# Differential attention in a written-out order, with pieces of the following products between its steps and fewer conditioning sums beside it

## Chip, cores and metric

The kernel runs on one core of one Trainium2 chip. The metric is the device time of one execution in microseconds (us), taken as the median of three runs.

## What is computed

The reference is two transformer blocks in a row on 256 tokens of width 1024, all in float32. The first block is a sparse-attention and convolution mixer and a SwiGLU. The second block has two layers of three sublayers: SwiGLU, mixer, SwiGLU; the mixer of its layer 0 is differential attention, that of layer 1 a gated recurrence. Each sublayer is modulated by shift, scale and gate vectors that are products of a conditioning vector `c` (1024) with a 1024x1024 matrix each, 24 vectors in all. Differential attention, cut to what matters here:

```python
q, k, v = jnp.split(h @ w_qkv, 3, axis=-1)
q = rms_norm(q.reshape(B, S, H, 2, hd), q_gain) * (hd ** -0.5)
k = rms_norm(k.reshape(B, S, H, 2, hd), k_gain)
...
s = jnp.einsum('bhcqd,bhckd->bhcqk', q_blk, kt).astype(jnp.float32) + bias[None, :, None]
s = jnp.where(dist >= 0, s, -jnp.inf)
p = jax.nn.softmax(s, axis=-1)
a = p[:, :, 0] - lam_full * p[:, :, 1]
return jnp.einsum('bhqk,bhkv->bhqv', a, vt)
...
o = rms_norm(o, subln_gain) * (1.0 - lambda_init)
return o.reshape(B, S, H * dv).astype(h.dtype) @ w_o
```

There are 8 heads with two 64-wide query and key halves each, and values of 128.

## The kernel before

**Products.** A float32 product is made of three matmuls on fp32r halves: weight high by activation high, weight low by activation high, weight high by activation low. `Stream` brings every weight matrix in chunks of 128x2048 through a pool of five raw buffers. For each half of a chunk ScalarE copies the high part (`whi`, L200) and VectorE subtracts it (`wlo`, L213); `Stream.next` hands out the two halves of a chunk, splits a number of halves ahead (`ahead`) and issues the loads of later chunks (`loads`) on SyncE's queue.

**Conditioning sums.** The 24 vectors come from 88 columns of 1 MB (`adaraw`) and the first block's own. `ADA_PLAN` is a table of (chunk number, columns loaded by then). `Stream.next` calls `ada_step` with the chunk number plus 8: at most one more column is loaded, into the same five raw buffers, and the sums of one earlier column are made, two VectorE passes over 128x1024 (L550, or L548 for the first). When four columns of a vector are there, `reduce` turns the sum on TensorE (L570 for a gate, L573 for a shift or scale) and VectorE takes it from PSUM (L579, L581).

**Order.** Between `order(True)` and `order(False)` instructions keep, on every engine, the order in which the Python code issues them; elsewhere the tile framework's list scheduler reorders them by its own costs. The first block, all SwiGLUs and the first part of the recurrence are in written order. `diff_attention` (L1673) calls `order(False)` at its start; `finish` (L795) puts the written order back on for the last half of the output product.

**The attention stage.** It has four groups `i` of two heads. The SwiGLU before it ends with the first group's query/key product (`rows_first`). For each group, `normed` squares the product `ps_qk` on ScalarE (`qsq`, L1693), sums on VectorE (`qss`, L1695), takes the power -1/2 on GpSimd (L630), multiplies (`qk`, L1699), turns on TensorE (`ps_qkT`, L1704), and ScalarE writes `qn` and `kn` (L1707). Then for each 128 queries `t` and each half `e`: scores on TensorE (`ps_s`, L1726), bias and row maximum on VectorE (L1729), exponentials with row sums on ScalarE (L1734); after both halves the difference `a` on VectorE (L1737 to L1741), turned on TensorE (`ps_aT`, L1744) and copied by ScalarE (`aT`, L1745). `rows_half` makes the next group's query/key product, and later the two halves of the values (`ps_v`), each from two weight chunks. Per half of the values, `ps_o` (L1755) and `head_norm` follow: square, sum, power, multiply, turn (`ps_oT`, L1794) and split; then the output product `ps_do` from four chunks (`out_product`, `finish`).

Of the kernel before, what the change touches and what calls it, by code (L numbers as in the profile page):

```python
# [413 lines left out]
class Net:  # L414
# [85 lines left out]
    ADA_PLAN = ((0, 0), (8, 0), (14, 12), (36, 24), (56, 36), (76, 48), (93, 60), (126, 72), (159, 84), (184, 84), (204, 88))  # L500
# [170 lines left out]
    def half_pieces(self, name, done):  # L671
        acc = [self.psum("acc", f"{name}{t}") for t in range(2)]
        xh, xl = self.h
        for j in range(2):
            parts = self.W.next(ahead=1)
            for k in range(4):
                f = 4 * j + k
                for t in range(2):
                    self.rows_mm([acc[t]], parts[k // 2], t, (xh[:, f], xl[:, f]), f == 0, f == KT - 1, (k % 2) * 512)
                if k == 2:  # L680
                    self.W.split_to(2 * self.W.at + 1)
                if f == KT - 1:
# [40 lines left out]
    def rows_part(self, acc, lhs, ks, first):  # L723

        parts = self.W.next()
        for a, k in enumerate(ks):
            for t in range(2):
                self.rows_mm(acc[t], parts[a], t, lhs(k), first and a == 0, False)

# [942 lines left out]
    def diff_attention(self, bias_pool, end, scale, fill):  # L1672
        nc, T, tc, W = self.nc, self.T, self.tc, self.W  # L1673
        with ExitStack() as es:
# [10 lines left out]
            s0 = m1.tile([P, 2, 8], F32, name="s0")  # L1685
            acc, base = self.started
            self.ada_step(base + 8)
            self.ada_step(base + 9)
            self.order(False)
            for i in range(4):  # L1690
                def normed(t, ps):
                    sq = self.w512("qsq")
                    nc.scalar.activation(sq, ps, AF.Square)  # L1693
                    ss = m2.tile([P, 8], F32, name="qss")
# [3 lines left out]
                    y = self.w512("qk").rearrange("p (a b) -> p a b", a=8)  # L1698
                    nc.vector.tensor_tensor(out=y, in0=ps.rearrange("p (a b) -> p a b", a=8),  # L1699
                                            in1=ss[:, :, None].to_broadcast([P, 8, 64]), op=ALU.mult)  # L1700
                    y = y.rearrange("p a b -> p (a b)")
                    pt = self.psum("t", "ps_qkT")
                    for k in range(4):
                        nc.tensor.transpose(pt[:, k * P:(k + 1) * P], y[:, k * P:(k + 1) * P], self.ident)  # L1704
                    pt = pt.rearrange("p (a b) -> p a b", a=4)
                    for dst, src, gn in ((qn, pt[:, :2], qg), (kn, pt[:, 2:], kg)):
                        nc.scalar.activation(dst[:, 2 * i:2 * i + 2, t * P:(t + 1) * P], src, AF.Copy, scale=gn)  # L1707

                if i == 0:
                    for t in range(2):  # L1710
                        normed(t, acc[t])
                else:
                    self.rows_half("ps_qk", normed)
                for t in range(2):
                    n = (t + 1) * P
                    pa = self.psum("t", "ps_aT")
                    s = [None] * 2
                    s1 = m2.tile([P, 2], F32, name="ds1")
                    for e in range(2):

                        ps = self.psum("b", "ps_s").rearrange("p (a b) -> p a b", a=2)[:, :, :n]
                        s[e] = self.w512("s").rearrange("p (a b) -> p a b", a=2)[:, :, :n]
                        nm = m2.tile([P, 2], F32, name="dnm")
                        for k in range(2):
                            h = 2 * i + k
                            nc.tensor.matmul(ps[:, k], qn[64 * e:64 * e + 64, h, t * P:(t + 1) * P], kn[64 * e:64 * e + 64, h, :n],  # L1726
                                             start=True, stop=True, tile_position=(64 * e, 0))
                        for k in range(2):
                            nc.vector.tensor_tensor_reduce(out=s[e][:, k], in0=ps[:, k], in1=bias[:, 2 * i + k, S - n:], scale=1.0,  # L1729
                                                           scalar=GONE, op0=ALU.add, op1=ALU.max, accum_out=nm[:, k:k + 1])  # L1730
                        nc.vector.tensor_scalar(out=nm, in0=nm, scalar1=-1.0, scalar2=None, op0=ALU.mult)
                        for k in range(2):
                            h = 2 * i + k
                            nc.scalar.activation(s[e][:, k], s[e][:, k], AF.Exp, bias=nm[:, k:k + 1],  # L1734
                                                 accum_out=s0[:, t, h:h + 1] if e == 0 else s1[:, k:k + 1])

                    nc.vector.reciprocal(s1, s1)  # L1737
                    nc.vector.scalar_tensor_tensor(out=s1, in0=s0[:, t, 2 * i:2 * i + 2], scalar=nlam, in1=s1, op0=ALU.mult, op1=ALU.mult)
                    for k in range(2):
                        a = self.w256("a")[:, :n]  # L1740
                        nc.vector.scalar_tensor_tensor(out=a, in0=s[1][:, k], scalar=s1[:, k:k + 1], in1=s[0][:, k], op0=ALU.mult, op1=ALU.add)  # L1741
                        for b in range(t + 1):
                            c = k * (t + 1) + b
                            nc.tensor.transpose(pa[:, c * P:(c + 1) * P], a[:, b * P:(b + 1) * P], self.ident)  # L1744
                    nc.scalar.copy(aT[:, 2 * i:2 * i + 2, t:2 * t + 1], pa[:, :2 * n].rearrange("p (a b c) -> p a b c", a=2, b=t + 1))  # L1745
            v = m1.tile([P, 2, D], F32, name="v", tag="v")
            oh, ol = m1.tile([P, KT, S], F32R, name="oh", tag="qn"), m1.tile([P, KT, S], F32R, name="ol", tag="kn")
            for g in range(2):
                self.rows_half("ps_v", lambda t, ps: nc.scalar.copy(v[:, t, g * 512:(g + 1) * 512], ps))
                for t in range(2):  # L1750
                    ps = self.psum("b", "ps_o")
                    for e in range(4):
                        h = 4 * g + e
                        for b in range(t + 1):
                            nc.tensor.matmul(ps[:, e * P:(e + 1) * P], aT[:, h, t + b], v[:, b, h * P:(h + 1) * P],  # L1755
                                             start=b == 0, stop=b == t)
# [260 lines left out]
```

## Time and profile before

| | |
|---|---|
| runs, us | 1455.15, 1457.65, 1460.42; median 1457.65 |
| profiled execution | 1461.74 us, its span 1459.9 us, granted TensorE clock 0.992 |
| busy share of the span | TensorE 97%, VectorE 75%, ScalarE 49%, GpSimd 3% |
| DMA | 61.8% of 16 engines, 230 GB/s from HBM |

TensorE (PE) is busy nearly all of the span, so a gain has to come from stretches where it waits or runs at its lower clock. A busy PE is modelled from pipelined matmuls: what a matmul costs is read from the distance of starts or from the time of a whole train, not from its own duration.

### The profile page before, as it was taken

Reading aid. Unit: us, or ns where it says so; the run is one execution under the profiler, and the core shown is the slowest. Engines: PE = TensorE matmul, PEld = TensorE weight load, DVE = VectorE, ACT = ScalarE, POOL = GpSimd, SP = SyncE. Lnnn points to the kernel's source line nnn. Section 1 sums busy time; section 2 is a strip of 40 time slices with the busy share of each in tenths; the row PEclk is TensorE's granted clock in tenths of the full one; section 3 lists DMA queues with packets and bytes.
Section 4 is the critical chain, followed back from the end, with each engine's and each line's share of the span. In section 5 each row is a group of like instructions: output and inputs, shape, how many; then the busy total and the mean of one; then the engine's idle time right before and its main releaser. Section 6 shows DMA issues by size and latency. Waiting matters only on the chain.

```text
span 1459.9 us, 22646 instructions
## 1 busy us (share of the span) xinstructions
PE 1409.4 (97%) x9154; PEld 1258.5 (86%) x9154; DVE 1095.0 (75%) x1691; ACT 709.0 (49%) x1217; POOL 47.2 (3%) x45
## 2 busy tenths in 40 slices
PE   7999999999999999889999999999998999999998
PEld 6875889998899897667999998999987998899997
DVE  4889797778797678889776668866676998765555
ACT  4544534444444446565544445444455675454442
POOL 0001000000000000122000000000000001000000
PEclk9999999999999999999999999999999999999999
DMA  7866588774588875766476764766653244266640
GB/s 280 329 271 231 212 348 309 270 296 179 193 332 337 327 283 188 253 224 221 148 314 233 279 256 159 301 260 255 232 187 143 91 145 170 90 222 247 235 173 30
DMA packets 51353, 337.87 MB, mean 231 GB/s; under 512 B 5760, under 2 KB 7552, under 8 KB 13104
## 3 DMA queue, kind: packets, MB, share of 16 engines
q1 hardware_dynamic: 51104, 336.35, 61.8%
q8 instruction: 72, 1.18, 0.3%
q14 instruction: 33, 0.27, 0.1%
q10 hardware_dynamic: 144, 0.07, 0.0%
HBM read 335.33 MB, written 1.06 MB: 230 GB/s over the span
## 4 chain that ended last, share of the span: by engine, by line
PE 78%; DVE 12%; ACT 3%; issue 3%; POOL 2%; DMA 1%; SPq 0%; POOLq 0%; DVEq 0%; ACTq 0%
PE ps_dn L692 19%; PE ps_up L654 13%; PE ps_up L656 13%; PE ps_up L653 13%; DVE wlo L213 2%; PE ps_up L888 2%; PE ps_wo L708 2%; PE ps_att L692 2%; DVE adacc L550 1%; POOL qss L630 1%; PE ps_up L901 1%; PE ps_do L692 1%; ACT whi L200 1%; PE ps_c L1150 1%; PE ps_g L692 1%
## 5 line engine op out<-in xcount | busy, mean ns | idle before, releaser
L213 DVE TENSOR_TENSOR wlo<-raw,whi 128x1024 fp32r<-128x1024 f32 (+2 forms) x414 | 484.8, 1207 | 48.9 <-ACT whi L200 48.3
L200 ACT CAST whi<-raw 128x1024 fp32r<-128x1024 f32 (+2 forms) x414 | 412.7, 1037 | 130.1 <-issue 44.1
L654 PE MATMUL ps_up<-xh,wlo 128*128 128x256 f32 x1600 | 392.4, 283 | 1.2 <-DVE wlo L213 1.2
L653 PE MATMUL ps_up<-xh,whi 128*128 128x256 f32 x1600 | 393.5, 284 | 0.0
L654 PEld LDWEIGHTS ps_up<-xh,wlo 128*128 128x128 f32 x1600 | 306.1, 191 | 4.4 <-DVE wlo L213 1.6
L653 PEld LDWEIGHTS ps_up<-xh,whi 128*128 128x128 f32 x1600 | 305.9, 191 | 3.3 <-ACT g L1001 0.9
L656 PE MATMUL ps_up<-xl,whi 128*128 128x256 f32 x1600 | 224.4, 283 | 0.0
L656 PEld LDWEIGHTS ps_up<-xl,whi 128*128 128x128 f32 x1600 | 206.2, 192 | 0.0
L550 DVE SCALAR_TENSOR_TENSOR adacc<-adaraw,cact,adacc 128x1024 f32<-128x1024 f32 x154 | 197.3, 1281 | 4.5 <-ACT adacc L545 1.6
L1001 ACT ACTIVATE g<-ps_up 128x256 f32<-128x256 f32 x100 | 38.4, 384 | 317.9 <-PE ps_up L656 317.9
L692 PE MATMUL ps_dn<-whi,hh 128*128 128x512 f32 x440 | 174.0, 395 | 0.0
L692 PE MATMUL ps_dn<-wlo,hh 128*128 128x512 f32 x440 | 172.7, 393 | 0.0
L1003 DVE TENSOR_TENSOR hu<-ps_up,g 128x256 f32<-128x256 f32 x100 | 42.2, 422 | 154.5 <-ACT g L1001 154.3
L692 PE MATMUL ps_dn<-whi,hl 128*128 128x512 f32 x440 | 140.7, 394 | 0.0
L692 PEld LDWEIGHTS ps_dn<-whi,hl 128*128 128x128 f32 x440 | 82.6, 188 | 18.6
L692 PEld LDWEIGHTS ps_dn<-whi,hh 128*128 128x128 f32 x440 | 83.1, 189 | 17.0 <-issue 0.2
L692 PEld LDWEIGHTS ps_dn<-wlo,hh 128*128 128x128 f32 x440 | 82.8, 188 | 17.3 <-issue 0.2
L637 DVE TENSOR_TENSOR hl<-hu,hh 128x256 fp32r<-128x256 f32 x100 | 42.5, 425 | 47.2 <-ACT hh L636 47.2
L636 ACT CAST hh<-hu 128x256 fp32r<-128x256 f32 x100 | 40.7, 407 | 61.9 <-DVE hu L1003 61.9
L630 POOL TENSOR_TENSOR rstd<-rstd,mhalf 128x1 f32<-128x1 f32 x16 | 10.0, 626 | 867.4 <-DVE rstd L303 642.6
L369 ACT ACTIVATE xh<-ps_tr,vcol,modA 128x128 fp32r<-128x128 f32 x48 | 18.0, 456 | 31.4 <-PE ps_tr L358 25.7
L1921 PE MATMUL ps_l<-hX 128*128 128x128 f32 x224 | 29.8, 276 | 0.2 <-DVE hX L1906 0.2
(340 smaller groups left out, 1869.3 us busy)
## 6 DMA issues: line engine op xcount, KB each, us to landing
raw<-in_up_dram SPq DMA_DIRECT2D x110, 1024.0 KB, 6.1
adaraw<-in_ada_dram SPq DMA_DIRECT2D x88, 1024.0 KB, 5.7
raw<-in_down_dram SPq DMA_DIRECT2D x55, 1024.0 KB, 6.8
adas<-in_ada_s_dram SPq DMA_DIRECT2D x8, 1024.0 KB, 4.9
raw<-in_w_qk_dram SPq DMA_DIRECT2D x8, 1024.0 KB, 7.1
raw<-in_w_att_dram SPq DMA_DIRECT2D x8, 724.0 KB, 6.2
wraw<-in_w_conv_dram SPq DMA_DIRECT2D x8, 512.0 KB, 11.0
gate<-in_ada_b_dram SPq DMA_DIRECT2D x8, 512.0 KB, 7.8
```

What stands on the lines that cost most here:

```text
L200: net.nc.scalar.copy(hi[:, :n], src)
L213: self.net.nc.vector.tensor_tensor(out=lo[:, :n], in0=src, in1=hi.bitcast(F32)[:, :n], op=ALU.subtract)
L550: nc.vector.scalar_tensor_tensor(out=acc, in0=raw[:, k], scalar=c[:, 2 * j + k:2 * j + k + 1], in1=acc, op0=ALU.mult, op1=ALU.add)
L636: nc.scalar.copy(hi, src)
L637: nc.vector.tensor_tensor(out=lo, in0=src, in1=hi.bitcast(F32), op=ALU.subtract)
L653: mm(o, hi[:, at(k)], xh[:, k], start=k == 0, stop=False)
L654: mm(o, lo[:, at(k)], xh[:, k], start=False, stop=False)
L656: mm(o, parts[k // 4][0][:, at(k)], xl[:, k], start=False, stop=k == KT - 1)
L692: mm = lambda *args, **more: self.nc.tensor.matmul(*args, **more, **kw)
L1001: self.last_silu = nc.scalar.activation(g, ps[:, :S], AF.Silu)
L1003: nc.vector.tensor_tensor(out=u, in0=ps[:, S:], in1=g, op=ALU.mult)
L1921: nc.tensor.matmul(pd[:, o:o + P], x, x, start=True, stop=True)
```

## The change

`diff_attention` no longer calls `order(False)`: the whole stage keeps the order of the code. `normed` is cut into `begin` and `turn`, the rest of a group into `scores` and `weights`, the part per values half into `averaged` and `ended` (`head_norm` now yields once, after the power). A query/key, value or output product is issued in eight pieces of six matmuls (`half_pieces`, which also splits weights between its pieces, and `rows_pieces`), and `plan` names the step that follows a piece. `ADA_PLAN` is flatter from chunk 76 to 94 and steeper after; the reduction of vector 16 moves from the attention to the SwiGLU behind it, and that of vector 19 one SwiGLU further. The parts that are only regrouped are cut.

```diff
-    ADA_PLAN = ((0, 0), (8, 0), (14, 12), (36, 24), (56, 36), (76, 48), (93, 60), (126, 72), (159, 84), (184, 84), (204, 88))
+    ADA_PLAN = ((0, 0), (8, 0), (14, 12), (36, 24), (56, 36), (76, 48), (86, 52), (94, 56), (131, 70), (160, 84), (184, 84), (204, 88))
...
-            parts = self.W.next(ahead=1)
+            parts = self.W.next(ahead=1, loads=3)
...
+    def rows_pieces(self, acc, lhs, ks, first):
 
         parts = self.W.next()
         for a, k in enumerate(ks):
             for t in range(2):
                 self.rows_mm(acc[t], parts[a], t, lhs(k), first and a == 0, False)
+                yield
...
-            self.order(False)
-            for i in range(4):
-                def normed(t, ps):
...
+            def begin(i):
+                for t in range(2):
                     sq = self.w512("qsq")
...
                     self.power(ss, ss)
...
+            def turn(i, t):
+                ss, ps = sums.pop((i, t)), accs[i][t]
...
+            def scores(i, t):
...
+            def weights(i, t):
...
+            def qk(i):
+                accs[i] = {}
+                return self.half_pieces("ps_qk", accs[i].__setitem__)
+
+            def value(g):
+                return self.half_pieces("ps_v", lambda t, ps: nc.scalar.copy(v[:, t, g * 512:(g + 1) * 512], ps))
+
+            def run(stream, plan):
+                for p, _ in enumerate(stream):
+                    for f, *args in plan.get(p, ()):
+                        f(*args)
...
+            for i in range(4):
+                begin(i)
...
+                plan = {2: [(turn, i, 0)], 4: [(turn, i, 1), (scores, i, 0)], 5: [(scores, i, 1)], 7: [(weights, i, 0)]}
+                if i:
+                    plan[1] = [(weights, i - 1, 1)]
+                run(qk(i + 1) if i < 3 else value(0), plan)
...
+            ended = lambda g, t: next(heads[g, t], None)
+            run(value(1), {0: [(averaged, 0, 0)], 1: [(weights, 3, 1)], 2: [(averaged, 0, 1)], 5: [(ended, 0, 0)], 7: [(ended, 0, 1)]})
...
+            run(self.rows_pieces(acc, lhs, (0, 1), True), {0: [(averaged, 1, 0)], 1: [(averaged, 1, 1)]})
+            run(self.rows_pieces(acc, lhs, (2, 3), False), {1: [(ended, 1, 0)], 3: [(ended, 1, 1)]})
+            self.finish(acc, lhs, range(4, 8), end, fill)
...
-            self.diff_attention(bp, End(self, 11, 1.0, self.mods(0, 2)), *early(16), early(15, 14))
+            self.diff_attention(bp, End(self, 11, 1.0, self.mods(0, 2)), early(15, 14))
...
-        self.ffn(2, End(self, 14, 0.5, self.mods(1, 0)), early(19), early(18, 17))
+        self.ffn(2, End(self, 14, 0.5, self.mods(1, 0)), early(16), early(18, 17))
...
-        self.ffn(3, End(self, 17, 0.5, self.mods(1, 1), mixer="ps_i"), early(22), early(21, 20))
+        self.ffn(3, End(self, 17, 0.5, self.mods(1, 1), mixer="ps_i"), early(19, 22), early(21, 20))
```

Three places of the instruction order follow, before and now. A number behind a name tells buffers apart.

VectorE (DVE) at the opening of the stage, from the last low halves of the modulated input (`xl`) on. Before:

```order
L389 TENSOR_TENSOR xl<-hf,xh 128x4x128 x2
L1695 TENSOR_REDUCE qss<-qsq 128x8
L1696 TENSOR_SCALAR qss<-qss 128x8
L1699 TENSOR_TENSOR qk<-ps_qk_5658,qss 128x512
L213 TENSOR_TENSOR wlo<-raw,whi 128x1024
L579 TENSOR_TENSOR gate<-ps_red,gate 128x512
```

Now:

```order
L389 TENSOR_TENSOR xl<-hf,xh 128x4x128 x2
L579 TENSOR_TENSOR gate<-ps_red,gate 128x512 x2
L581 TENSOR_REDUCE vcol<-ps_red 128x4 x2
L585 TENSOR_TENSOR vcol<-vcol,cols 128x8
L550 SCALAR_TENSOR_TENSOR adacc<-adaraw,cact,adacc 128x1024 x4
L1698 TENSOR_REDUCE qss<-qsq 128x8
L1699 TENSOR_SCALAR qss<-qss 128x8
L1698 TENSOR_REDUCE qss<-qsq 128x8
L1699 TENSOR_SCALAR qss<-qss 128x8
L1771 SCALAR_TENSOR_TENSOR nlam<-lams 128x1
L213 TENSOR_TENSOR wlo<-raw,whi 128x1024 x4
L1705 TENSOR_TENSOR qk<-ps_qk_5654,qss 128x512
```

The first split of the second group's weights (`wlo`) and the first `qk` now stand behind two gate adds, two reductions and four passes of conditioning sums.

ScalarE (ACT) from a group's exponentials to the next group's. Before, behind group 0:

```order
L200 CAST whi<-raw 128x1024 x2
L1693 ACTIVATE qsq<-ps_qk_5887 128x512
L1745 COPY aT<-ps_aT 128x2x256
L200 CAST whi<-raw 128x1024 x2
L1693 ACTIVATE qsq<-ps_qk_5888 128x512
L1707 ACTIVATE qn<-ps_qkT,cols 128x2x128
```

Now:

```order
L1734 ACTIVATE s,s_5774<-s,dnm 128x128 x2
L1734 ACTIVATE s,ds_5881<-s,dnm 128x128 x2
L1734 ACTIVATE s,s_5774<-s,dnm 128x256 x2
L1734 ACTIVATE s,ds_5908<-s,dnm 128x256 x2
L200 CAST whi<-raw 128x1024
L1750 COPY aT<-ps_aT 128x2x128
L1696 ACTIVATE qsq<-ps_qk_5797 128x512
L1696 ACTIVATE qsq<-ps_qk_5798 128x512
L200 CAST whi<-raw 128x1024
L1750 COPY aT<-ps_aT 128x2x256
L200 CAST whi<-raw 128x1024
L1713 ACTIVATE qn<-ps_qkT,cols 128x2x128
```

One `whi` now stands behind each thing that ScalarE takes from TensorE or VectorE, where before they went in pairs.

VectorE in the same stretch, from a group's last score to the turn of its weights. Before (group 1):

```order
L1731 TENSOR_SCALAR dnm_6055<-dnm_6055 128x2
L213 TENSOR_TENSOR wlo_6123<-raw_6114,whi_6122 128x1024
L1695 TENSOR_REDUCE qss_6152<-qsq_6150 128x8
L1737 RECIPROCAL ds1_6042<-ds1_6042 128x2
L213 TENSOR_TENSOR wlo_6251<-raw_6114,whi_6250 128x1024
L1738 SCALAR_TENSOR_TENSOR ds1_6042<-s0_5781,nlam_5776,ds1_6042 128x2
L1696 TENSOR_SCALAR qss_6152<-qss_6152 128x8
```

Now (group 0):

```order
L213 TENSOR_TENSOR wlo_5936<-raw_5809,whi_5935 128x1024
L1742 RECIPROCAL ds1_5881<-ds1_5881 128x2
L1743 SCALAR_TENSOR_TENSOR ds1_5881<-s0_5774,nlam_5775,ds1_5881 128x2
L1746 SCALAR_TENSOR_TENSOR a_5948<-s_5893,ds1_5881,s_5883 128x128
L1746 SCALAR_TENSOR_TENSOR a_5951<-s_5893,ds1_5881,s_5883 128x128
L1698 TENSOR_REDUCE qss_5957<-qsq_5955 128x8
L1699 TENSOR_SCALAR qss_5957<-qss_5957 128x8
L1698 TENSOR_REDUCE qss_5963<-qsq_5961 128x8
L1699 TENSOR_SCALAR qss_5963<-qss_5963 128x8
L213 TENSOR_TENSOR wlo_5972<-raw_5811,whi_5971 128x1024
L1742 RECIPROCAL ds1_5908<-ds1_5908 128x2
```

Every step of the weights (`a`) now has a `wlo` directly ahead of it on VectorE.

## Rows read from the trace of the kernel before

**Rows 1.** The page, part 1: busy us, share of the span, instructions.
```profile
PE 1409.4 (97%) x9154; PEld 1258.5 (86%) x9154; DVE 1095.0 (75%) x1691; ACT 709.0 (49%) x1217; POOL 47.2 (3%) x45
```

**Rows 2.** Stretches: length, busy PE, PEld, DVE, ACT, POOL, granted clock, DMA share, GB/s.
```profile
579.50:700.20 120.70, 109.65 (x541) 83.61 (x540) 106.96 (x240) 65.90 (x141) 25.56 (x13) 0.97 0.64 227
...
1110.00:1190.00 80.00, 74.30 (x591) 72.84 (x592) 66.20 (x119) 50.45 (x103) 0.00 (x0) 0.96 0.31 108
```

**Rows 3.** PE's waits, 560 to 705 us: us, times, longest.
```profile
PE ps_qkT L1704 <- DVE qk L1699: 3.8, 4, 1.4
PE ps_aT L1744 <- DVE a L1741: 3.3, 3, 1.8
```

**Rows 4.** The chain that ended last, whole trains on PE: start, us, what.
```profile
689.78 10.41 PE ps_do L692 x45
...
707.50 0.87 PE ps_red L573 x8
...
814.16 5.58 PE ps_dn L692 x24
```

**Rows 5.** Timeline of PE in the stage: start, us, instruction.
```profile
579.51 1.88 PE L570 MATMUL ps_red<-adacc,ones 128*128 128x512 f32 x4
...
597.56 0.80 PE L692 MATMUL ps_qk<-wlo,xh 128*128 128x512 f32 x1 [0.72 <-DVE wlo L213]
...
602.42 0.57 PE L692 MATMUL ps_qk<-wlo,xh 128*128 128x512 f32 x1
...
613.42 0.72 PE L1726 MATMUL ps_s<-kn,qn 64*128 64x128 f32 x8
...
617.89 1.14 PE L1726 MATMUL ps_s<-kn,qn 64*128 64x256 f32 x8
```

**Rows 6.** Instruction groups of the stage, shapes apart: busy us, mean ns, idle before.
```profile
L213 DVE TENSOR_TENSOR wlo<-raw,whi 128x1024 fp32r<-128x1024 f32 x27 | 32.6, 1215 | 0.0
L200 ACT CAST whi<-raw 128x1024 fp32r<-128x1024 f32 x28 | 29.3, 1048 | 23.2 <-PE ps_do L692 7.6 <-PE ps_qk L692 6.5 <-PE ps_v L692 4.4
L550 DVE SCALAR_TENSOR_TENSOR adacc<-adaraw,cact,adacc 128x1024 f32<-128x1024 f32 x19 | 24.3, 1277 | 0.0
...
L1734 ACT ACTIVATE s<-s,dnm 128x256 f32<-128x256 f32 x16 | 8.0, 502 | 1.6 <-DVE dnm L1731 1.6
L1729 DVE CUSTOM_DVE_ANT_0 s<-ps_s,biasT 128x256 f32<-128x256 f32 x16 | 6.4, 415 | 0.0
L1699 DVE TENSOR_TENSOR qk<-ps_qk,qss 128x512 f32<-128x512 f32 x8 | 5.5, 691 | 11.0 <-POOL qss L630 11.0
L1695 DVE TENSOR_REDUCE qss<-qsq 128x8 f32<-128x512 f32 x8 | 5.4, 677 | 0.1
L1693 ACT ACTIVATE qsq<-ps_qk 128x512 f32<-128x512 f32 x8 | 4.7, 593 | 1.5 <-PE ps_qk L692 1.5
L1707 ACT ACTIVATE qn<-ps_qkT,cols 128x256 f32<-128x256 f32 x8 | 3.8, 476 | 12.1 <-PE ps_qkT L1704 12.1
L1741 DVE SCALAR_TENSOR_TENSOR a<-s,ds 128x256 f32<-128x256 f32 x8 | 3.5, 475 | 0.0
L1745 ACT COPY aT<-ps_aT 128x512 f32<-128x512 f32 x4 | 2.3, 586 | 2.8 <-PE ps_aT L1744 2.8
L1738 DVE SCALAR_TENSOR_TENSOR ds<-s,nlam,ds 128x2 f32<-128x2 f32 x8 | 1.7, 214 | 0.0
...
L1745 ACT COPY aT<-ps_aT 128x256 f32<-128x256 f32 x4 | 1.4, 362 | 0.2
```

**Rows 7.** Timeline of DVE: a waiting instruction and the one behind it.
```profile
615.33 0.69 DVE L1699 TENSOR_TENSOR qk<-ps_qk,qss 128x512 f32<-128x512 f32 x1 [1.53 <-POOL qss L630]
615.93 0.28 DVE L1729 CUSTOM_DVE_ANT_0 s<-ps_s,biasT 128x128 f32<-128x128 f32 x1
```

**Rows 8.** DMA issues: KB each, median us to landing.
```profile
adaraw<-in_ada_dram SPq DMA_DIRECT2D x88, 1024.0 KB, 5.7
...
raw<-in_w_qk_dram SPq DMA_DIRECT2D x8, 1024.0 KB, 7.1
```

More of the change, by code (lines that the diff above doesn't have):

```diff
@@ L728, in rows_part @@
                 self.rows_mm(acc[t], parts[a], t, lhs(k), first and a == 0, False)
+                yield
+    def rows_part(self, *args):
+        for _ in self.rows_pieces(*args):
+            pass
     def order(self, on):
@@ L1670, in attention_setup, with diff_attention @@
         yield
[L1672 removed]
+    def diff_attention(self, bias_pool, end, fill):
         nc, T, tc, W = self.nc, self.T, self.tc, self.W
@@ L1697, in normed @@
                     self.power(ss, ss)
[L1698 to L1704, printed above, removed]
@@ L1746, in diff_attention @@
-            v = m1.tile([P, 2, D], F32, name="v", tag="v")
-            oh, ol = m1.tile([P, KT, S], F32R, name="oh", tag="qn"), m1.tile([P, KT, S], F32R, name="ol", tag="kn")
[L1748 to L1756, printed above, removed]
-                    r = m2.tile([P, 4], F32, name="dr")
-                    nc.vector.tensor_tensor(out=r, in0=s0[:, t, 4 * g:4 * g + 4], in1=s0[:, t, 4 * g:4 * g + 4], op=ALU.mult)
-                    self.head_norm(m2, ps, t, g, r, 128 * EPS2, None, [sg] * 4, oh, ol)
+            def turn(i, t):
+                ss, ps = sums.pop((i, t)), accs[i][t]
+                y = self.w512("qk").rearrange("p (a b) -> p a b", a=8)
+                nc.vector.tensor_tensor(out=y, in0=ps.rearrange("p (a b) -> p a b", a=8),
+                                        in1=ss[:, :, None].to_broadcast([P, 8, 64]), op=ALU.mult)
+                y = y.rearrange("p a b -> p (a b)")
+                pt = self.psum("t", "ps_qkT")
+                for k in range(4):
+                    nc.tensor.transpose(pt[:, k * P:(k + 1) * P], y[:, k * P:(k + 1) * P], self.ident)
+                pt = pt.rearrange("p (a b) -> p a b", a=4)
+                for dst, src, gn in ((qn, pt[:, :2], qg), (kn, pt[:, 2:], kg)):
+                    nc.scalar.activation(dst[:, 2 * i:2 * i + 2, t * P:(t + 1) * P], src, AF.Copy, scale=gn)
@@ new lines, in weights @@
+            def weights(i, t):
+                n = (t + 1) * P
+                p0, p1, s1 = probs.pop((i, t))
+                pa = self.psum("t", "ps_aT")
+                nc.vector.reciprocal(s1, s1)
+                nc.vector.scalar_tensor_tensor(out=s1, in0=s0[:, t, 2 * i:2 * i + 2], scalar=nlam, in1=s1, op0=ALU.mult, op1=ALU.mult)
+                for k in range(2):
+                    a = self.w256("a")[:, :n]
+                    nc.vector.scalar_tensor_tensor(out=a, in0=p1[:, k], scalar=s1[:, k:k + 1], in1=p0[:, k], op0=ALU.mult, op1=ALU.add)
+                    for b in range(t + 1):
+                        c = k * (t + 1) + b
+                        nc.tensor.transpose(pa[:, c * P:(c + 1) * P], a[:, b * P:(b + 1) * P], self.ident)
+                nc.scalar.copy(aT[:, 2 * i:2 * i + 2, t:2 * t + 1], pa[:, :2 * n].rearrange("p (a b c) -> p a b c", a=2, b=t + 1))
@@ new lines, in diff_attention, with averaged @@
+            oh, ol = m1.tile([P, KT, S], F32R, name="oh", tag="qn"), m1.tile([P, KT, S], F32R, name="ol", tag="kn")
+            def averaged(g, t):
+                ps = self.psum("b", "ps_o")
+                for e in range(4):
+                    h = 4 * g + e
+                    for b in range(t + 1):
+                        nc.tensor.matmul(ps[:, e * P:(e + 1) * P], aT[:, h, t + b], v[:, b, h * P:(h + 1) * P],
+                                         start=b == 0, stop=b == t)
+                r = m2.tile([P, 4], F32, name="dr")
+                nc.vector.tensor_tensor(out=r, in0=s0[:, t, 4 * g:4 * g + 4], in1=s0[:, t, 4 * g:4 * g + 4], op=ALU.mult)
+                heads[g, t] = self.head_norm(m2, ps, t, g, r, 128 * EPS2, None, [sg] * 4, oh, ol)
+                next(heads[g, t])
```

81 lines of the change are left out of this document (34 added, 47 removed).

## Prediction

> **What bounds the kernel now.** I began with the page's first part. PE is busy 97% of the span, DVE 75% [rows 1]: on average nothing but PE's work can be cut, and the change cuts none. So I looked for a stretch where PE waits. The table by stretch shows it in the attention stage, from the end of the first query/key product (579.5 us) to the end of the output product (689.78 + 10.41 = 700.2) [rows 2, 4]: 120.7 us in which PE counts 109.65 busy, at a granted clock of 0.97, while DVE is busy 106.96. The reader is to see two things there: PE's gaps are short, and DVE is nearly as full as PE. PE's list of waits names DVE for them: 3.8 us for `qk`, 3.3 for `a` [rows 3].
>
> A busy PE is modelled, so I count its work anew. 336 products 512 wide are 14 trains of 24, each 5.58 us [rows 4]: 78.1. 88 transposes, eight in 0.87 [rows 4]: 9.6. Two gate sums: 1.88 [rows 5]. Scores, four times 0.72 + 1.14 [rows 5]: 7.4. The 48 passes of `ps_o`, which I take to cost a transpose each: 5.2. That is 102.2 us of work, so 18.5 of the 120.7 are waits, changes between kinds of matmul, and slow clock. **18.5 us is the most that a better order can give**, 1.3% of the kernel.
>
> **The change, part by part.** What moves without a price: the turn of vector 16, eight transposes or 0.9 us on PE [rows 4], leaves the stage and comes back in the next SwiGLU, where PE is the bound too: sum zero. The flatter plan takes DVE passes out of the stage, 22 before (19 [rows 6] and three first passes), 14 now; the eight others go to SwiGLUs, whose VectorE has room (75% over the kernel [rows 1]), at no cost. If that room were missing, 8 x 1.28 = 10.2 us would be the bound. The larger `loads` issues transfers earlier; nothing in the ring below waits for one.
>
> What counts is the order. Each engine now takes its instructions as the code issues them. I walked the queues from one PE event to the next, with each duration from its group [rows 6]; PE's cover is pieces of six products, 5.58 / 4 = 1.395 us each [rows 4].
>
> *A, turn of `a` for t=0.* It stands behind the scores of t=1 and two pieces: 1.14 + 2.79 = 3.9 us of cover. The way to it: half the scores 0.57, four score passes on DVE 4 x 0.415, the last two exponentials 2 x 0.50, then `whi` 1.05 and `wlo` 1.215 because they were issued ahead, `a` 0.475, and three two-column steps of 0.21: 6.6. PE waits 2.7.
>
> *B, turn of `a` for t=1,* two pieces later (2.8): copy of `aT` 0.36, two squares 1.19, `whi` 1.05, `wlo` 1.215, two small steps 0.43, `a` 0.475: 4.7. Wait 1.9.
>
> *C, first turn of `qk`,* one piece later (1.4): `aT` copy 0.59, `whi`, `wlo`, `qk` 0.69: 3.55. Wait 2.15.
>
> *D, second turn of `qk`,* two pieces later (2.8): `qn` and `kn` 0.95, `whi`, `wlo`, `qk`: 3.9. Wait 1.1.
>
> That is 7.85 us per group. It comes back each time, since each way starts at PE's last turn: a ring. GpSimd's power is ready before in each case. Three full rings: 23.6. In two of them two conditioning passes (2 x 1.28, less 0.2 of slack) stand ahead of B's `wlo`: 4.7. The last A: 2.7.
>
> *Opening.* DVE used to split the next weights at once; now four reductions and adds (0.68 each), four conditioning passes (5.1), two sums of squares (1.8 with their small steps) and one `wlo` come first: 10.8 us from 580.45, so 591.3. PE is through with its conditioning turns at 579.51 + 1.88 + 0.87 = 582.3 [rows 4, 5]. Wait 9.0. The third piece of weights is loaded into the buffer that the second of those passes frees at 585.7, lands 7.1 us later [rows 8], and with `whi`, two `wlo` and `qk` the first turn comes at 597.0, PE at 595.5: 1.5. The second turn waits for a column whose buffer the second `wlo` frees at 592.5: plus 5.7 [rows 8], two passes, `wlo`, `qk`: 602.65, PE at 600.2: 2.4. Opening 12.9.
>
> *Tail.* The values' second half and the first output chunks hold four more waits of the same make. I don't walk them: A to D lie between 1.1 and 2.7, I take 1.8 each, 7.2, with 0 and 11 as ends.
>
> Waits now: 12.9 + 23.6 + 4.7 + 2.7 + 7.2 = 51.1. Stage: 102.2 - 0.9 + 51.1 = 152.4 against 120.7, so +31.7, and +0.9 in the SwiGLU. Steps on one engine overlap a little (615.33 + 0.69 ends after 615.93 [rows 7]): 25 places of 0.09, -2.2. **+30.4 us.** The profiled execution took 1461.74, so 1492.1; the median lies 4.1 below it, so **1488**.
>
> **Does a waiting instruction hold those behind it?** All of the ring hangs on that. Row: at 615.33 DVE had stood idle 1.53 us for GpSimd's power, though scores that PE began at 613.42 and that took 0.72 lay ready; it read them at 615.93, right behind the `qk` that it waited for [rows 5, 7]. So it holds them. The Trainium skill, Perfetto Trace Analysis, in its section on the Tensor Engine Instruction, says that VectorE, ScalarE and GpSimd are strict first-in first-out; by that rule every wait above stands, and if an engine could pass a waiting `wlo`, the result would be the gain of rival 1 instead. The trace agrees, with its 1.53 us.
>
> **Rivals.**
>
> 1. *DVE's load was the bound, and the pieces cover the rest: faster.* PE waits for DVE [rows 3], and DVE loses eight passes or 10.2 us; if the splits are made before PE needs them, the stage shrinks by that: 1447 (all waits gone: 1439). For it: a hand-ordered stretch of the recurrence keeps PE busy 74.3 of 80 us [rows 2]. Against: it needs way A within 3.9 us; without `whi` and `wlo` it is 4.35, with them 6.6. Chance 0.15.
>
> 2. *The slow clock follows the waits.* Behind gaps around 596 us, 12 products took 602.42 - 597.56 = 4.9 us instead of 2.8 [rows 5], starts twice as far apart, so 1.2 instead of 2.4 GHz: 2.1 us lost. One such spell per ring, at the opening and at the end adds up to 10: 1498, two per ring 1506. For it: PE would work only two thirds of the stage. Against: longer PE work also covers part of the ways. Chance 0.12. The Trainium skill, TensorE: Matmul & The Clock Gate, in its section on what's actually happening, says that the low rate is the default and sustained activity lifts it; by that the long wait of the opening costs a spell and the short ones need not. No run shows yet which.
>
> 3. *The ring is shorter.* Each way 0.5 us shorter on twelve ways, and the opening's transfers land 3 us earlier: -9 to -20: 1468 to 1479. Chance 0.10.
>
> 4. *No change:* what the order loses, the freed DVE gives back, within 0.3% (4.4 us, about what a measurement of this kernel can tell from no change). Chance 0.05. That the order isn't really fixed I give nothing: the listing shows it.
>
> **How the numbers follow.** The forecast, 1478 to 1497, has 0.58; the rest as above. Slower by over 0.3%: 0.58 + 0.12 + 0.10 = 0.80; within 0.05; faster 0.15. The range leaves out rivals 1 and 4 or a part of 2, 0.2 in all: 1460 to 1508.
>
> **What would show it.** In the new profile the stage from the first query/key product to the output product is about 150 us long and PE's list of waits in it sums to 40 or more, led by `ps_aT` on `a`, `ps_qkT` on `qk`, and one wait of 8 to 9 us on the first `wlo` of `ps_qk`; ScalarE's `whi` and DVE's `wlo` stand directly ahead of each; DVE's 11.0 us for GpSimd [rows 6] is nearly gone. The SwiGLUs keep their time but for 0.9. It would be wrong if PE's waits stayed under 20 us, if the opening's wait were under 3, or if a SwiGLU or the recurrence changed by more than 2 us.

## The result, and the profile after

The changed kernel takes **1499.3 us** (median of 4 runs, 1496.4 to 1499.9) against 1458.1 for the kernel before (4 runs beside it, 1455.2 to 1460.4): 1.028 times as long, 95% interval 1.0266 to 1.0297, so 41 us slower. The forecast was 1488, its likeliest case 1478 to 1497, its range 1460 to 1508.

Where the time went: the attention stage. First PE's line of the page, then the stage's row of the table by stretch (from, to, length; busy us of PE, weight loads, DVE, ACT, POOL; granted clock; DMA share, GB/s), both to be read beside [rows 1, 2].

```profile
PE 1414.6 (94%) x9154; PEld 1259.8 (84%) x9154; DVE 1102.5 (74%) x1691; ACT 709.2 (47%) x1217; POOL 40.8 (3%) x45
```
```profile
576.34:736.90 160.56, 118.86 (x534) 89.66 (x532) 105.20 (x232) 67.31 (x144) 20.39 (x13) 0.89 0.41 148
```

The stage lasts 160.6 us instead of 120.7: +39.9 (in the two profiled executions, whose spans differ by 38.2). DVE has no more to do than before (105.2 against 106.96), and PE's busy time is longer (118.9 against 109.65) while its clock is lower, 0.89 against 0.97. What lies outside the stage is 1337.5 us long against 1339.2; the profiles of the change and its six variants by hand below, which differ only inside the stage, differ by up to 2.5 us ahead of it and as much behind it, so nothing more is to be read from that, the 0.9 us of vector 16 included. From the end of the stage to the end of the next SwiGLU it is 194.2 us in the kernel before and 194.4 now; the SwiGLU after that takes 194.3 and 195.1, and from there to the last `ps_dn`, with the recurrence, it is 366.8 and 367.3.

PE's list of waits in the stage (us in all, times, longest), the answer to [rows 3]:

```profile
PE ps_aT L1749 <- DVE a L1746: 21.0, 8, 3.4
PE ps_qkT L1710 <- DVE qk L1705: 8.9, 6, 2.2
PE ps_qk L692 <- DVE wlo L213: 8.7, 1, 8.7
PE ps_oT L1832 <- DVE on L1823: 2.9, 3, 2.1
```

With 0.2 for a gate these are 41.7 us; before, the same list sums to 11.0. One full ring on PE's timeline, with the wait ahead of each turn in brackets: A, B, C and D in this order.

```profile
633.67 0.66 PE L1749 MATMUL ps_aT<-ident,a 128*128 128x128 f32 x2 [3.39 <-DVE a L1746]
...
641.07 0.74 PE L1749 MATMUL ps_aT<-ident,a 128*128 128x128 f32 x4 [2.85 <-DVE a L1746]
...
645.39 0.63 PE L1710 MATMUL ps_qkT<-ident,qk 128*128 128x128 f32 x4 [2.20 <-DVE qk L1705]
...
649.84 0.63 PE L1710 MATMUL ps_qkT<-ident,qk 128*128 128x128 f32 x4 [1.08 <-DVE qk L1705]
```

What stands ahead of the next A is on ACT's and DVE's timelines. `a` for t=0 is 0.61 us of work behind two small steps, and its inputs are ready once ACT has read out the last sum of t=0, at 653.41 + 0.19 = 653.60. It comes only at 659.62: behind its score passes DVE holds at a `wlo` (2.21 us idle), and that `wlo` needs a `whi` that ACT began only behind the exponentials of t=1 as well, at 656.97:

```profile
653.41 0.19 ACT L1734 ACTIVATION_READ_ACCUMULATOR s<-s,dnm 128x1 f32 x1
...
656.88 0.18 ACT L1734 ACTIVATION_READ_ACCUMULATOR s<-s,dnm 128x1 f32 x1
656.97 1.03 ACT L200 CAST whi<-raw 128x1024 fp32r<-128x1024 f32 x1
```
```profile
658.03 1.23 DVE L213 TENSOR_TENSOR wlo<-raw,whi 128x1024 fp32r<-128x1024 f32 x1 [2.21 <-ACT whi L200]
659.17 0.16 DVE L1742 RECIPROCAL ds<-ds 128x2 f32<-128x2 f32 x1
659.36 0.22 DVE L1743 SCALAR_TENSOR_TENSOR ds<-s,nlam,ds 128x2 f32<-128x2 f32 x1
659.62 0.61 DVE L1746 SCALAR_TENSOR_TENSOR a<-s,ds 128x128 f32<-128x128 f32 x2
```

And this is PE behind that wait, from its timeline and from the table by stretch: matmuls start 0.43 us apart, not 0.23, so at 1.2 GHz, until about 664.

```profile
660.12 0.50 PE L1749 MATMUL ps_aT<-ident,a 128*128 128x128 f32 x2 [3.40 <-DVE a L1746]
660.37 0.65 PE L692 MATMUL ps_v<-whi,xh 128*128 128x512 f32 x1
660.82 0.63 PE L692 MATMUL ps_v<-wlo,xh 128*128 128x512 f32 x1
661.25 0.63 PE L692 MATMUL ps_v<-whi,xl 128*128 128x512 f32 x1
...
664.10 0.40 PE L692 MATMUL ps_v<-whi,xh 128*128 128x512 f32 x1
664.33 0.39 PE L692 MATMUL ps_v<-wlo,xh 128*128 128x512 f32 x1
```
```profile
656.00:660.00 4.00, 0.72 (x4) 0.26 (x2) 1.90 (x5) 2.00 (x6) 0.00 (x0) 1.00 0.01 2
660.00:664.00 4.00, 3.88 (x11) 3.08 (x12) 2.61 (x6) 2.29 (x4) 1.40 (x1) 0.57 0.79 262
```

Cut into such rows of 4 us, the stage has eight with a granted clock under 0.8 in which PE works; PE's busy time in each row times the share of the clock that is missing sums to 11.8 us. The stage before, cut the same way, gives 2.8. So of the +39.9, 30.7 are waits and 9.0 are slow clock; 0.2 are left, the difference of 0.9 less for vector 16's turn and 1.1 more that I can't place.

DVE's groups show the same from the other side: `wlo`, which waited 0.0 before, stands idle 27.4 us for `whi`, and the 11.0 us that DVE waited for GpSimd's power ahead of `qk` [rows 6] are gone.

```profile
L213 DVE TENSOR_TENSOR wlo<-raw,whi 128x1024 fp32r<-128x1024 f32 x28 | 33.7, 1222 | 27.4 <-ACT whi L200 27.4
...
L1705 DVE TENSOR_TENSOR qk<-ps_qk,qss 128x512 f32<-128x512 f32 x8 | 5.5, 683 | 0.0
```

### The profile page after: what moved, and what is told of

Its sections match the earlier page's. It is cut to its first block, busy times and chain, and to the rows that moved or that the text cites. A ratio compares the mean times of both kernels' runs of the same rounds, so it can differ in the third digit from the quotient of the medians.

```text
span 1498.1 us, 22650 instructions
## 1 busy us (share of the span) xinstructions
PE 1414.6 (94%) x9154; PEld 1259.8 (84%) x9154; DVE 1102.5 (74%) x1691; ACT 709.2 (47%) x1217; POOL 40.8 (3%) x45
## 4 chain that ended last, share of the span: by engine, by line
PE 74%; DVE 13%; ACT 6%; issue 3%; DMA 3%; POOL 1%; SPq 0%; POOLq 0%; ACTq 0%; DVEq 0%
PE ps_dn L692 19%; PE ps_up L656 12%; PE ps_up L654 12%; PE ps_up L653 12%; DVE wlo L213 3%; PE ps_up L893 2%; PE ps_wo L708 2%; ACT whi L200 2%; DVE adacc L550 1%; DMA adas<-in_ada_s_dram 1%; PE ps_up L906 1%; PE ps_qk L692 1%; PE ps_g L692 1%; PE ps_red L570 1%; PE ps_do L692 1%
## 5 line engine op out<-in xcount | busy, mean ns | idle before, releaser
L692 PEld LDWEIGHTS ps_dn<-whi,hl 128*128 128x128 f32 x440 | 82.6, 188 | 18.6
```

Of the source, the lines that this page charges most:

```text
L692: mm = lambda *args, **more: self.nc.tensor.matmul(*args, **more, **kw)
```

## The experiments

My theory after the result: the fixed order of the queues makes the ring of waits, and the waits bring the slow clock. Rivals: the plan of conditioning sums, the pieces themselves, DVE's load as a whole, the transfers. All stages below run from the first gate sum to the end of `ps_do`; lines move by a few between kernels.

### The parts of the change, one by one

**plan_only**: the kernel before, with the new plan of sums and the turns of vectors 16 and 19 that go with it, and nothing else of the change. Here and below the diffs are cut at the dots; the last dots stand for the two moved turns.

```diff
-    ADA_PLAN = ((0, 0), (8, 0), (14, 12), (36, 24), (56, 36), (76, 48), (93, 60), (126, 72), (159, 84), (184, 84), (204, 88))
+    ADA_PLAN = ((0, 0), (8, 0), (14, 12), (36, 24), (56, 36), (76, 48), (86, 52), (94, 56), (131, 70), (160, 84), (184, 84), (204, 88))
...
-            self.diff_attention(bp, End(self, 11, 1.0, self.mods(0, 2)), *early(16), early(15, 14))
+            self.diff_attention(bp, End(self, 11, 1.0, self.mods(0, 2)), None, early(15, 14))
...
```

> The kernel before with the change's plan of conditioning sums alone: fewer VectorE passes in the attention stage, the turns of vectors 16 and 19 in later SwiGLUs, the stage's order as it was. Theory Q (the order in each engine's queue is what cost the 41 us; the plan is harmless): 1446 to 1460 us, the stage 110 to 122 us long; at best the eight freed passes, 10.2 us. Rival P (the plan is the cost: the passes crowd the SwiGLUs, or vectors 16 and 19 come late there): 1470 to 1498, with the time added in the second or third SwiGLU and not in the stage.

Measured: 1454.8 us, 0.9984 of before (0.9975 to 0.9993). The stage is 117.4 us long. The plan is not the cause.

**fixed_before**: plan_only with the stage's order fixed by hand as its code is written, no pieces.

```diff
-            self.order(False)
             for i in range(4):
                 def normed(t, ps):
```

> The kernel before with the change's plan of conditioning sums (as plan_only) and, in the stage, the order in which its own code is written, fixed by hand as in the change, but without the change's pieces: steps between whole products, nothing put between. Theory Q: the fixed queues are what costs, and the pieces give part of it back, so this is slower than the change: per pair of heads PE would stand still for the whole chain from the square of ps_qk to the turn of a, some 15 us in place of 7.9; 1520 to 1560 us. Rival U (the pieces themselves, with the splits spread over them, are what costs): 1455 to 1490, faster than the change.

**own_order**: the changed kernel, with the order in the stage given back to the scheduler.

```diff
             accs, sums, probs = {0: acc}, {}, {}
+            self.order(False)
```

> The changed kernel, pieces and plan, with the stage's order left to the scheduler again as in the kernel before (the output product's end stays by hand, as there). Theory Q: without the fixed queues the stage goes back to 110 to 122 us and the time to 1448 to 1462 us. Rival U (the regrouping into pieces costs by itself, in whatever order): 1480 to 1500.

Measured: fixed_before 1553.7 us (1.066, 1.063 to 1.068), own_order 1450.1 (0.993, 0.991 to 0.996). With plan_only and the change itself that is a table of four, all with the new plan:

| | whole products | pieces |
|---|---|---|
| scheduler's order | 1454.8 | 1450.1 |
| order by hand | 1553.7 | 1499.3 |

The order by hand costs 99 us without pieces and 49 with them; the pieces gain in both rows. Theory Q holds, rival U falls. "Pieces" takes in what `half_pieces` brings along, later splits (`ahead=1`) and earlier loads (`loads=3`); no run takes these apart. In the stage's rows of fixed_before and own_order the second number is the length, 216.0 and 108.8; fixed_before has PE at a clock of 0.74, own_order loses none:

```profile
578.60:794.62 216.02, 128.92 (x535) 99.86 (x534) 107.97 (x233) 69.30 (x143) 17.69 (x13) 0.74 0.30 110
```
```profile
579.77:688.58 108.81, 104.41 (x533) 81.72 (x532) 92.36 (x223) 65.67 (x141) 22.29 (x13) 1.00 0.55 194
```

### What the conditioning passes cost in the fixed order

**no_sums**: the passes of seven steps of the plan, 13 of the stage's 14, cut to eight columns, so that the kernel leaves out most of these sums.

```diff
+                m = 8 if 49 <= n < 56 else D
-                nc.vector.scalar_tensor_tensor(out=acc, in0=raw[:, k], scalar=c[:, 2 * j + k:2 * j + k + 1],
-                                               in1=acc, op0=ALU.mult, op1=ALU.add)
+                nc.vector.scalar_tensor_tensor(out=acc[:, :m], in0=raw[:, k, :m], scalar=c[:, 2 * j + k:2 * j + k + 1],
+                                               in1=acc[:, :m], op0=ALU.mult, op1=ALU.add)
```

> The changed kernel with 13 of the stage's conditioning passes on VectorE cut from 1024 columns to 8; the sums of two conditioning vectors are left out for the rest, transfers and buffers stay as they are. Theory Q: the wait of the opening falls from 8.7 us by the four passes that stood ahead of the first wlo, 5.1 us, to about 3.6; B's second and third wait fall from 2.9 to about 0.5; the waits of A and C, which no pass stands ahead of, stay at 3.4 and 2.2; with one or two spells of slow clock fewer 1482 to 1491 us. Rival V (VectorE's load as a whole bounds the stage, wherever the passes stand): the stage shrinks by all 13 x 1.28 = 16.6 us and more, A and C's waits with it: under 1480. Rival W (the opening waits for transfers of weights): the opening's wait stays over 7, time above 1494.

Measured: 1490.1 us, 9.2 less than the change. DVE is busy 91.6 us in the stage instead of 105.2, and the stage shrinks by 9.7 to 150.9: less than the 13.6 that DVE lost. PE's waits:

```profile
PE ps_aT L1750 <- DVE a L1747: 16.2, 7, 3.4
PE ps_qkT L1711 <- DVE qk L1706: 9.7, 6, 2.2
PE ps_qk L693 <- DVE wlo L213: 4.5, 1, 4.5
```

The opening fell from 8.7 to 4.5, B's second wait from 2.85 to 1.34 and its third from 2.93 to nothing; A (3.4) and C's first two (2.2) stayed. Apart from changes of 0.4 us and less, only waits with a pass ahead of them fell; C's third grew from 1.3 to 2.2 and D's first from nothing to 1.1, to what C and D are elsewhere. That is theory Q, though the opening came out 0.9 above its 3.6; V and W fall.

### Moving the splits, or what waits behind them

**behind**: splits moved from ahead of A and B to behind a step.

```diff
-            parts = self.W.next(ahead=1, loads=3)
+            parts = self.W.next(ahead=0, loads=3)
...
-                if k == 2:
-                    self.W.split_to(2 * self.W.at + 1)
                 yield
+                if f == 1:
+                    self.W.split_to(2 * self.W.at)
+                if f in (2, 7):
+                    self.W.split_to(2 * self.W.at + 1)
...
-                plan = {2: [(turn, i, 0)], 4: [(turn, i, 1), (scores, i, 0)], 5: [(scores, i, 1)], 7: [(weights, i, 0)]}
+                plan = {2: [(turn, i, 0)], 4: [(turn, i, 1), (lambda: W.split_to(2 * W.at),), (scores, i, 0)], 5: [(scores, i, 1)], 7: [(weights, i, 0)]}
...
```

> The changed kernel with each weight split moved from ahead of a step to behind the step before or after it: none stands any more between the score passes and the turn of a (A, B), while one stays ahead of each turn of qk (C, D). Theory Q: the waits of ps_aT for a fall from 21.0 us in eight to under 6 (A's way is 6.6 - 1.05 - 1.215 = 4.3 us against 3.9 of cover, B's 2.4 against 2.8), the waits of ps_qkT for qk stay between 7 and 11; with two to four spells of slow clock fewer 1472 to 1486 us. Rival R (the places of the steps between the pieces are too early whatever stands in the queues, so that the splits only wait elsewhere): the waits of a stay above 15 or turn up ahead of the products that take the splits; 1495 to 1505.

Measured: 1502.0 us (1.030, 1.029 to 1.032), no better than the change. My number was wrong, rival R's right:

```profile
PE ps_aT L1751 <- DVE a L1748: 15.5, 4, 5.0
PE ps_qk L694 <- DVE wlo L213: 8.7, 1, 8.7
PE ps_qkT L1712 <- DVE qk L1707: 6.7, 4, 3.6
PE ps_oT L1834 <- DVE on L1825: 4.6, 3, 3.5
PE ps_s L1728 <- DVE dnm L1731: 4.2, 3, 1.4
```

A's four waits are gone (four of eight are left on `a`), but ahead of B there still stands a split, which the edit was meant to take away: behind A's `a` DVE is idle for its `whi`.

```profile
632.23 0.61 DVE L1748 SCALAR_TENSOR_TENSOR a<-s,ds 128x128 f32<-128x128 f32 x2
634.97 1.23 DVE L213 TENSOR_TENSOR wlo<-raw,whi 128x1024 fp32r<-128x1024 f32 x1 [2.12 <-ACT whi L200]
```

So B's way is no shorter than in the change (in the second ring 7.4 us from PE's first product behind A to B, against 7.1), while PE's two pieces ahead of it, no longer slow behind a wait for A, cover 3.0 us of it instead of 4.2. B's longest wait grew from 2.9 to 5.0, and the split behind D stands ahead of the scores: 4.2 us that weren't there. The sum of waits went from 41.7 to 39.9, but the stage is 167.3 us long, at a granted clock of 0.83. I had walked each way by itself; here a split that was moved along a full queue only changed whom it delayed.

So the next three leave the splits and bring what PE turns out ahead of them. **qk_early**: both `qk` right behind B, PE's turns where they were.

```diff
-            def turn(i, t):
+            def scaled(i, t):
...
+            def turn(i, t):
+                y = ys.pop((i, t))
...
-                if i:
-                    plan[1] = [(weights, i - 1, 1)]
+                plan[1] = [(weights, i - 1, 1)] * (i > 0) + [(scaled, i, 0), (scaled, i, 1)]
```

> The changed kernel with one thing moved: both VectorE products qk of a pair of heads are issued right behind a's products for t=1 (B), one and three pieces before PE turns them; splits, conditioning passes and PE's order as they are. Theory Q2 (work taken out of the chain between two PE events shortens the ring by itself): the waits of ps_qkT for qk, 8.9 us, fall to under 2, the others stay (A 3.4, B 2.9, the opening 8.7), with up to two spells of slow clock fewer: 1486 to 1492 us. Rival K (the ring keeps its sum, as it did in the run behind: the 1.4 us of qk now stand ahead of the splits and the scores): the waits come back at the scores or at a, 1496 to 1502.

**a_early**: both `a` right behind the scores.

```diff
-            def weights(i, t):
+            def mixed(i, t):
...
+            def weights(i, t):
+                a = mix.pop((i, t))
...
-                plan = {2: [(turn, i, 0)], 4: [(turn, i, 1), (scores, i, 0)], 5: [(scores, i, 1)], 7: [(weights, i, 0)]}
+                plan = {2: [(turn, i, 0)], 4: [(turn, i, 1), (scores, i, 0)], 5: [(scores, i, 1), (mixed, i, 0), (mixed, i, 1)], 7: [(weights, i, 0)]}
```

> The changed kernel with one thing moved: both VectorE products a of a pair of heads are issued right behind the scores of t=1, ahead of the split that stood before A, and so before B's split and passes; PE's order as it is. Theory Q2: A's way is 6.6 - 1.05 - 1.215 = 4.3 us against 3.9 of cover, B's operand is ready: the waits for a fall from 21.0 us to under 5; two conditioning passes now stand ahead of C's split in two rings, so that the waits for qk grow from 8.9 to 10 to 13; two to four spells of slow clock fewer: 1475 to 1487 us. Rival K (the ring keeps its sum): waits for a and qk together still over 25, 1495 to 1502.

Measured: qk_early 1487.8 us (1.021, 1.019 to 1.022), a_early 1477.5 (1.014, 1.012 to 1.015), both where Q2 put them. PE's waits, qk_early first:

```profile
PE ps_aT L1752 <- DVE a L1749: 22.0, 8, 3.4
PE ps_qk L692 <- DVE wlo L213: 8.7, 1, 8.7
```
```profile
PE ps_qkT L1710 <- DVE qk L1705: 12.7, 4, 4.9
PE ps_qk L692 <- DVE wlo L213: 8.7, 1, 8.7
```

Each takes away its own wait and leaves the other's: `qk` from 8.9 to none while `a` stays at 22.0; `a` from 21.0 to none while `qk` grows to 12.7, since the conditioning passes that stood ahead of B now stand ahead of C. Rival K falls.

**operands** does both, puts the splits and passes behind, and makes the first split of the stage ahead of the sums of squares. Of PE's turns of `a` and `qk` only A is a piece later, and D a piece earlier (a turn of `ps_oT` also comes two pieces earlier); the words "one piece later each" in the expectation are wrong in that.

```diff
-                plan = {2: [(turn, i, 0)], 4: [(turn, i, 1), (scores, i, 0)], 5: [(scores, i, 1)], 7: [(weights, i, 0)]}
+                plan = {0: [(first,)], 1: [(scaled, i, 0)], 2: [(turn, i, 0), (scaled, i, 1), (second,)],
+                        3: [(turn, i, 1), (third,)], 4: [(scores, i, 0)], 5: [(scores, i, 1), ADA, ADA],
+                        6: [(mixed, i, 0), (mixed, i, 1), (second,)]}
...
+                    plan[0].insert(0, (weights, i - 1, 0))
+                    plan[1].insert(0, (weights, i - 1, 1))
...
```

> The changed kernel, order still by hand, with what each turn reads made ahead of the splits: both qk and both pairs of a are issued one to two pieces before PE turns them, the turns one piece later each, the splits and conditioning passes behind them, and the first split ahead of the opening's sums of squares. Theory Q2 (after the run behind: within a fixed ring a moved split only makes the next one wait, and only work taken out of the chain between two PE events shortens it): waits for a and qk fall from 29.9 us to under 10, the opening's 8.7 to under 4, spells of slow clock to three or fewer; stage 115 to 135 us, time 1452 to 1473. Rival R2 (VectorE's and ScalarE's queues are so full that the waits come back at the scores or at the products that need a split): 1480 to 1500, with waits of ps_s or of ps_qk on wlo of 15 us and more.

Measured: 1466.4 us (1.006, 1.004 to 1.008): 33 of the 41 us are back, in the range of Q2. Its waits:

```profile
PE ps_aT L1754 <- DVE a L1745: 6.9, 4, 3.2
PE ps_qkT L1710 <- DVE qk L1702: 4.1, 4, 2.0
PE ps_oT L1845 <- DVE on L1836: 3.8, 2, 3.3
PE ps_qk L690 <- DVE wlo L213: 1.9, 1, 1.9
```

`a` and `qk` together are 11.0, a little over the 10 expected, and the opening 1.9. The order is still by hand, so 33 of the 41 us are not the price of a fixed order as such, but of what stands ahead of what in it. How much each of its parts gives isn't told apart, but for a_early's 22 us and qk_early's 12, each alone.

### The slow clock by itself

**dummies**: PE gets work in its waits.

```diff
+                    for _ in range((0 if k else 28) if t == 0 else (0 if k else 22)):
+                        nc.tensor.transpose(pa[:, 3 * P:], self.ident, self.ident)
...
+                for _ in range(0 if t else 16):
+                    nc.tensor.transpose(pt[:, 3 * P:], self.ident, self.ident)
```

> The changed kernel with idle PE work put into the waits: 28 more transposes of the identity ahead of each turn of a for t=0, 22 ahead of each for t=1, 16 ahead of each first turn of qk, overwritten afterwards; 264 transposes of 0.109 us, 28.8 us of work that nobody needs, in waits that sum to about 27. Theory S (the waits let the clock fall, and the slow spells of about 2 us each behind them are a cost of their own, some 16 us in the stage): the spells in the rings go, and the time falls in spite of the added work: 1484 to 1495 us, the clock in the stage from about 0.89 to 0.97 and more. Rival T (the slow spells have another cause, or are short because of it): the added work costs what overshoots the waits, 1499 to 1508, the spells stay.

Measured: 1498.1 us (1.028, 1.027 to 1.030), and the stage's row:

```profile
573.88:735.67 161.79, 138.69 (x798) 111.69 (x796) 105.08 (x232) 67.35 (x144) 20.40 (x13) 0.97 0.41 147
```

264 transposes more, 28.8 us of work for nothing, and the stage is 1.2 us longer. PE's waits fell from 41.7 to 23.1, by 18.6, so 28.8 - 18.6 = 10.2 us of the work were not covered, and 9.0 of these came back, nearly all from the clock: in rows of 4 us the loss fell by 8.8, from 11.8 to 3.0 us, all of it in the opening, where no transposes were put. So the spells in the rings come from PE standing idle: S was right on the mechanism, but its loss of some 16 us was too large and the time lies above its range of 1484 to 1495. Not every wait brings a spell of its own: the one of the tail went as well, though its wait got no transposes and stayed at 2.06 us (2.07 in the change):

```profile
706.26 0.63 PE L1836 MATMUL ps_oT<-ident,on 128*128 128x128 f32 x4 [2.06 <-DVE on L1827]
```

The Trainium skill, TensorE: Matmul & The Clock Gate, in its section on what's actually happening, says that the low rate is the default and activity lifts it; these rows agree, with a clock of 0.97 in the stage where the change has 0.89.

### A version that beats both

**own_order_5** is own_order again; **own_old_plan** has the old plan of sums too, and the turns of vectors 16 and 19 where they were, so that of the whole change only the pieces are left (with their `ahead=1` and `loads=3`), in the scheduler's order.

```diff
-    ADA_PLAN = ((0, 0), (8, 0), (14, 12), (36, 24), (56, 36), (76, 48), (86, 52), (94, 56), (131, 70), (160, 84), (184, 84), (204, 88))
+    ADA_PLAN = ((0, 0), (8, 0), (14, 12), (36, 24), (56, 36), (76, 48), (93, 60), (126, 72), (159, 84), (184, 84), (204, 88))
...
+            self.order(False)
...
+            self.reduce_now(16)
             self.finish(acc, lhs, range(4, 8), end, fill)
...
```

> The run own_order again, in more rounds beside the next one: it measured 1450.1 us, 0.9934 of the kernel before. Theory Q: 1446 to 1454 us, a gain of 0.3 to 0.8%. Rival (the first value was a fortunate set of runs): within 0.3% of the kernel before.

> The pieces with the scheduler's own order, as own_order, but with the plan of conditioning sums of the kernel before, vector 16's turn back in the stage and vectors 19 and 22 as before: of the change only the pieces are left. Theory Q with a gain of its own for the pieces and for the plan: own_order gained 8 us and the plan alone 2.6, so 1451 to 1457 us. Rival Z (the plan is what lets the pieces gain, since VectorE is full in the stage without it): 1456 to 1464 us, no faster than the kernel before.

Measured: own_order_5 1450.8 us (0.9954, 0.9941 to 0.9967), own_old_plan **1445.1** (0.992, 0.991 to 0.993), 12 us faster than before and 54 faster than the change. Rival Z falls, and the old plan is better here by 5.7 us than the new one; Q had it worse or equal, and its range is missed on the fast side. The stage and PE's waits for `a` in own_old_plan:

```profile
579.75:683.94 104.19, 103.73 (x541) 81.86 (x540) 101.49 (x235) 65.51 (x141) 20.75 (x13) 1.00 0.68 243
```
```profile
PE ps_aT L1750 <- DVE a L1747: 0.5, 2, 0.3
```

104.2 us with 0.5 of waits: PE is at work from end to end, and DVE is busy 101.5 of it. Why the scheduler fills PE better with more passes in the stage (own_order's second profile has a stage of 110.5 us and 5.7 of waits) is open; it wasn't tried.

## Why the prediction was right, and where its sum was off

- **Bound and ceiling.** 102.2 us of PE work in the stage, so 18.5 us to gain at most. own_old_plan's profile bears it out: 104.2 long, 16.5 less than in the profile before (the kernel's median gained 12). The count was 1.5 short (104.2 less 0.5 of waits is 103.7).
- **Plan of sums at no cost.** Right: plan_only is 2.6 us faster, not slower. That the new plan costs 5.7 beside own_old_plan, in the scheduler's order with pieces, was not foreseen.
- **Ring.** Right in kind and place; its terms, forecast and measured: A 2.7 and 3.4 (four times); B 1.9, or 4.3 with passes ahead, and 0.4, then 2.9 twice; C 2.15 and 2.2, 2.2, 1.3; D 1.1 and 0, 1.1, 1.1. For the three rings, the passes and the last A, 31.0 us forecast and 27.6 measured. A's way, from PE's scores to the turn, was 7.5 us (601.51 to 608.99) where the walk had 6.6. B came out shorter because PE's products ahead of it ran at the low clock and covered more of the way: in the first ring its way was 5.0 us (4.7 forecast), of which they covered 4.6 and not 2.8. qk_early shows the same way with the products at full clock, 0.23 us apart, and there the wait is 2.0:

```profile
605.99 0.48 PE L692 MATMUL ps_qk<-whi,xh 128*128 128x512 f32 x1
...
608.39 0.39 PE L692 MATMUL ps_qk<-wlo,xh 128*128 128x512 f32 x1
608.62 0.39 PE L692 MATMUL ps_qk<-whi,xl 128*128 128x512 f32 x1
611.00 1.08 PE L1752 MATMUL ps_aT<-ident,a 128*128 128x128 f32 x4 [1.99 <-DVE a L1749]
```

- **Opening.** 12.9 forecast, 9.8 measured (8.7 and 1.1): the wait of 9.0 for the first `wlo` was right, the term of 1.5 for weights that land late was nothing, and the 2.4 for a column that lands late came to 1.1, which was a wait for `whi` like D's and not for a transfer. **Tail.** 7.2 forecast, 4.1 measured.
- **The step that was mis-sized** is "PE's work 102.2, the rest waits". Waits were put at 51.1 and came to 41.7, 9.4 less; what is neither work nor wait was put at nothing (less 2.2 of overlap) and came to 160.6 - 101.3 - 41.7 = 17.6 us, of which 11.8 are slow clock; of the other 5.8, 1.5 are the work counted short, and the rest isn't placed. The row of before held that term already: of its 18.5 us only 11.0 were waits and 7.5 the rest, 2.8 of it clock, and I let it vanish instead of grow. The two errors offset each other in part, the more so as slow products shortened waits, and the time came out 11 us over the forecast, above the likeliest case's 1497. Rival 2 had this: one spell in each ring, at the opening and the end, 10 us. It was not an alternative to the ring but its companion, and belonged in the sum. Its price was read a little low: the products that start from 597.56 to 602.42 are twelve, but the thirteenth starts at 602.84 (the line below), so twelve took 5.3 us, and the spell cost 2.5. That 1499.3 lies next to its 1498 is partly luck: that sum has the waits 9.4 too long and five spells where there were eight. And the sentence that the short waits need not cost a spell was wrong here: seven of the eight spells stand behind waits of 2.07 to 3.4 us.

```profile
602.84 0.39 PE L692 MATMUL ps_qk<-whi,xl 128*128 128x512 f32 x1
```

- **Rival 1** (DVE's load was the bound) fell with the result and with no_sums. **Rival 3** (a shorter ring) had its part in the 9.4 at the opening (3.1) and the tail (3.1); in the ring the ways weren't shorter, the cover was longer. **What would show it**: stage 160 for "about 150", waits 41.7 for "40 or more", the leaders as named, DVE's wait for GpSimd ahead of `qk` gone, the SwiGLUs and the recurrence within 0.8 us.

## What to carry to other kernels

When you fix an order by hand, ask at each PE step what the engine that feeds it issues just ahead of the operand, and issue the operand first: bulk work with slack (weight splits, conditioning passes) belongs behind small work without any. Moving the bulk work along the queue only changed whom it delayed, and with two engines both nearly full, pieces for a scheduler to interleave were worth 12 us here, while the best order by hand that was tried lost 8. And where PE waits, add what the clock may lose behind the wait.

## What the runs showed of the hardware

Ten waits of the changed kernel's stage are 2.07 us or longer, and eight of them were followed by a spell at 1.2 GHz; my likeliest case had counted none. Length alone doesn't decide: waits of 2.85 and 2.20 us had no spell behind them, nor had one of 3.41 us in qk_early, and that of 2.07 us had one in the change and none in dummies (2.06). 264 transposes that nobody needs, put into the waits, cost the stage 1.2 us instead of 28.8. And the lower clock was partly free: it lengthened products whose end PE would else have spent waiting, so that B's first wait was 0.4 us where with products at full clock, in qk_early, it was 2.0.
